# Regrouping the small matmuls of each expert in a mixture-of-experts block

## The chip, the cores and the metric

The kernel runs on one core of a Trainium2 chip. The time is device time in microseconds (us) of one execution, the median of three runs. The program is one launch.

## The reference, cut to what matters

The block is one layer of an encoder over 512 tokens of 1024 features in f32: pooling and differential attention, cross attention over 256 memory tokens, and then the part that the change touches, a mixture of 32 experts of which each token takes four:

```python
logits = (xt @ w_router + b_router)
top_val, top_idx = lax.top_k(logits, 4);  gates = softmax(top_val)
# for each expert e, on the tokens that chose it:
gu = xb @ w_gu[e] + b_gu[e]                      # (tokens, 2048)
gate, up = minimum(gu[:, :1024], 7), clip(gu[:, 1024:], -7, 7)
hb = (up + 1) * gate * sigmoid(1.702 * gate)     # (tokens, 1024)
yb = (hb @ w_down[e] + b_down[e]) * gate_of_token
y  = zeros.at[token].add(yb);   x = x + y;   out = rms_norm(x, g)
```

An expert has 64 tokens on average (512 x 4 / 32), and its weights are 12 MB, read once.

## The kernel before

The dense part fills the first 390 us or so; the change leaves it alone. The experts follow, in `experts` (L1173), one iteration per expert, and a last iteration (e = 32) for what is left.

An expert has up to 96 slots for its tokens: the first 64, and 32 more that run only if more than 64 tokens chose it. That choice is a branch at run time (`when`, L100, on a bit of a word that TensorE's sequencer has loaded; called `cond` in the loop). Experts with more than 96 tokens are finished by a loop at the end (`overflow`). An expert with over 64 tokens is called full in the prediction.

The products are in f32 with tokens as the columns of the weights' side: 64 slots take 64 columns of the array, and two such matmuls, for two halves of the output, stand beside each other in it; 32 slots take 32 columns, and four stand beside each other. `gate_up1` (L1086) is the product of one of eight pieces of the contraction in 64 columns, `gate_up2` (L1093) in 32. `down` (L1116) has `first(h)` in 64 columns for two halves h of the contraction, and `second(q, b)` in 32 columns for eight pieces.

Around these stand small jobs of TensorE, all with 128 columns:

- the slots (S): `dispatch` (L983) turns the places of the tokens into one-hots on VectorE and multiplies; out come the token numbers and gates of an expert's slots, which VectorE picks up in seven small instructions (`slots`, L966). The token rows are then gathered by an indirect DMA (`gather`, L989) into one buffer, and scaled on ScalarE (`normed`, L996);
- the transposes of the gathered tokens (T1): `to_features` (L1002), eight transposes into two banks, which VectorE writes to `xT` with the norm's gain in two halves; gate-up reads `xT`;
- the transposes of the activations (T2): `turn_act` (L1099), four and two, copied to `aT` by ScalarE; down reads them;
- the biases of gate-up (B): `biases` (L1068), four matmuls that start the sums;
- the pair's sums: `combine` (L1156). The outputs of down are split into two parts by `split` (L113), a ScalarE copy and then a VectorE subtraction for each piece, and kept for two experts (a pair). Then, for each of four blocks of 128 tokens, six matmuls with one-hots add the pair's outputs into two banks (`sum_up`), and VectorE adds these to x (`add_sums`, L1169).

The order on TensorE is the order of the program: `queued` (L88) hangs each matmul behind the one before it, branches included. On the other engines the framework's scheduler fixes an order ahead of time, from its own estimate of when each instruction is ready, the earlier one in the program first among the ready ones. Loads of weights are issued on the SP queue: `load_gate_up(e + 1)` and `load_down(e)` at the start of an iteration, each as soon as one of 17 buffers of 1 MB is free.

PSUM has eight banks: four single ones (`bank`, L137: slots, transposed activations, the 32-column part of gate-up, both parts of down), and two pairs (`pair`, L140: the 64-column part of gate-up, T1, and the sums).

Iteration e before the change, on TensorE: B; gate-up of 64 columns for pieces 0 to 7, with S (of expert e + 2) after piece 2, the first half of the 32-column part (if the expert is full) after piece 3, and T2 of expert e - 1 after piece 6. If e is odd and over 2, one of the four blocks of the sums of the last complete pair stands after each of the pieces 3 to 6. Then the second half of the 32-column part, T1 of expert e + 1, and down of expert e - 1: `first(0)`, the 32-column part, `first(1)`. In expert 1 the gate-weighted biases of down go into x in the places of the sums (`down_biases`, L944, then `combine`).

Of the kernel before, what the change touches and what calls it, by code (L numbers as in the profile page):

```python
# [15 lines left out]
OP = mybir.AluOpType  # L16
# [4 lines left out]
P = 128  # L21
D = 1024
S = 512
NT = S // P
KT = D // P
MEM = 256
NE = 32
# [33 lines left out]
class Block:  # L61
# [1054 lines left out]
    def down(self, aT, aT2, dn, gat, tok, cond, a, c, last=False):  # L1116


        (ya, oha), (yb, ohc) = a, c
        nc, mw = self.nc, self.mw  # L1120
        pd = [self.bank("down1") for _ in range(2)] if last else [self.bank("down1")] * 2
        pe = self.bank("down2", (P, 256))

        def first(h):
            for c in range(4):
                w = dn[2 * h + c // 2]
                for o in range(2):
                    k = D * (c % 2) + 512 * o
                    self.mm(pd[o][64 * o:64 * o + 64], aT[:, c, 64 * h:64 * h + 64], w[:, k:k + 512],
                            start=h == 0 and c == 0, stop=h == 1 and c == 3, skip_group_check=True)  # L1130

        def second(q, b):
            for o in range(4):
                k = D * b + 256 * o
                self.mm(pe[32 * o:32 * o + 32], aT2[:, b, 32 * q:32 * q + 32], dn[q][:, k:k + 256],
                        start=q + b == 0, stop=q == 3 and b == 1, skip_group_check=True)

        nc.vector.tensor_scalar(oha, self.iota_t, tok[:, 0:1], None, op0=OP.is_equal)
        nc.vector.tensor_scalar(ohc, self.iota_t[0:64], tok[0:64, 1:2], None, op0=OP.is_equal)
        if not last:  # L1140
            first(0)
        second(0, 0)
        with cond():
            for k in range(1, 8):
                second(k // 2, k % 2)
        for q in range(4):
            r, c = slice(32 * q, 32 * q + 32), slice(256 * (q % 2), 256 * (q % 2) + 256)
            self.split(yb[0:32, q // 2, c], yb[32:64, q // 2, c], pe[r], scale=gat[r, 1:2])
        if last:
            first(0)  # L1150
        first(1)
        for h in range(2):
            r = slice(64 * h, 64 * h + 64)
            self.split(ya[0:64, h], ya[64:P, h], pd[h][r], scale=gat[r, 0:1])

    def combine(self, i, parts):  # L1156

        nc = self.nc
        self.add_sums(i, self.sum_up(i, self.pair("comb"), parts, True, True))

    def sum_up(self, i, ps, parts, start, stop):
        t = slice(i * P, (i + 1) * P)
# [10 lines left out]
    def experts(self):  # L1173
        nc = self.nc
        disp, xTs, xgs = {}, {}, {}

        def gather(e):
            xgs[e] = self.gather(disp[e][0])

        def slots(e):  # L1180
            return [t[:, 0] for t in disp[e][1:]]

        xTs[0] = self.first_features()
        acts, parts = {}, {}
        pick = self.pick.rearrange("p v h q e -> p (v h q) e")
        for e in range(NE + 1):

            if e < NE:
                gu = self.gu.pop(e)
                cond = lambda e=e: self.when(self.flag(e))  # L1190
                if e == 0:
                    biases = self.load_down_biases()
                if e + 1 < NE:
                    self.load_gate_up(e + 1)
                    if e:
                        gather(e + 1)
                self.load_down(e)
                xT = xTs.pop(e)
                pa, pc = self.biases(pick[:, :, e:e + 1])
                for j in range(KT):  # L1200
                    self.gate_up1(pa, xT, gu[j], j)
                    if e == 0 and j == 0:
                        self.count()
                    if e == 0 and j == 1:
                        disp[1] = self.dispatch(1, 1)
                        gather(1)
                    if j == 3 or e == 0 and j in (1, 5):
                        with cond():
                            for k in range(j - 1 if e == 0 else 0, j + 1):
                                self.gate_up2(pc, xT, gu[k], k)  # L1210
                    if j in (3, 4, 5, 6) and e % 2 and e > 2:
                        self.combine(j - 3, parts[e // 2 - 1])
                    if j == 2 and e + 2 < NE:
                        disp[e + 2] = self.dispatch(e + 2, 1)
                    if j == 5 and e == 0:
                        disp[0] = self.dispatch(0, 1)
                        biases = self.round_down_biases(biases)
                    if e == 1 and j == 2:
                        biases = self.down_biases(biases)
                    if e == 1 and 2 < j < 7:  # L1220
                        self.combine(j - 3, [biases])
                    if j == 6 and e >= 1:
                        aT = [self.turn_act(t, n) for t, n in zip(acts.pop(e - 1), (4, 2))]
                    if j == 6 and e + 1 < NE:
                        xg = self.normed(xgs.pop(e + 1))
                if e:
                    act = self.swiglu(pa[:, 0], pa[:, 1], 512)
                with cond():
                    for k in range(4 if e else 6, KT):
                        self.gate_up2(pc, xT, gu[k], k)  # L1230
                if e == 0:
                    xTs[1] = self.to_features(xg)
                    act = self.swiglu(pa[:, 0], pa[:, 1], 512)
                acts[e] = act, self.swiglu(pc[:, 0], pc[:, 1], 256)
                if 0 < e < NE - 1:
                    xTs[e + 1] = self.to_features(xg)
            else:
                aT = [self.turn_act(t, n) for t, n in zip(acts.pop(e - 1), (4, 2))]

            if e:  # L1240
                f = e - 1
                r = slice(64 * (f % 2), 64 * (f % 2) + 64)
                if f % 2 == 0:
                    parts[f // 2] = self.sums()
                p = parts[f // 2]
                self.down(*aT, self.dnw.pop(f), *slots(f), lambda f=f: self.when(self.flag(f)),
                          p[2 * (f % 2)], [t[r] for t in p[1]], last=e == NE)
        self.finish(parts[NE // 2 - 1])
        self.overflow()
# [151 lines left out]
```

## Time and profile before

| what | us |
|---|---|
| median of 3 runs | 1530.26 (1529.31 to 1531.73) |
| the profiled execution | 1531.06 |
| its span, first to last instruction | 1529.3 |
| TensorE (PE) busy | 1482.5 (97% of the span) |
| weight loads (PEld) busy | 748.6 (49%) |
| VectorE (DVE) busy | 695.2 (45%) |
| ScalarE (ACT) busy | 385.1 (25%) |
| GpSimd (POOL) busy | 39.0 (3%) |

How to read it: the span is one execution; the time of an execution is a little longer. Busy time of an engine is the union of its instructions, and the matmuls' ends are modelled, so that a busy TensorE says that it has a matmul under way, not that it does as much as it could. A run of matmuls of one tile on the timeline is one row; an f32 matmul leaves two records in it. Idle time in brackets is that of the engine ahead of the row, with what ended it; PEq is TensorE's sequencer (here the branch).

### The profile page before, as it was taken

The page shows a single profiled execution, that of the slowest core. Times are in us where ns is not written, and L with a number is a line of the kernel's source. Part 1 is how long each engine was busy: PE and PEld are TensorE (multiplying, and loading weights), DVE is VectorE, ACT ScalarE, POOL GpSimd, SP SyncE. Part 2 cuts the span into 40 slices and gives each one's busy share as a digit, 9 for nine tenths or more (in the row PEclk, how much of TensorE's full clock was granted, in tenths as well). Part 3 has the DMA queues.
Part 4 walks back from the last instruction along what each step waited for, and adds up shares of the span by engine and source line. Part 5 has one row for each costly group of instructions (what it writes and reads, how often), then busy time and mean ns, then how long its engine had stood idle before and what let it go on. Part 6 is the DMA issues. An engine that isn't in the chain of part 4 may idle for free. (4 is left out here: it accounts for less than half of the span.)

```text
span 1529.3 us, 22025 instructions
## 1 busy us (share of the span) xinstructions
PE 1482.5 (97%) x8852; PEld 748.6 (49%) x8852; DVE 695.2 (45%) x1679; ACT 385.1 (25%) x691; POOL 39.0 (3%) x52
## 2 busy tenths in 40 slices
PE   8999999999999999999999999999999999999994
PEld 7878788888433333434333333333343433433332
DVE  6858865543353433335343334344343433444234
ACT  5346644441111111121211112121111112121113
POOL 0000000000000000000000000000000000000001
PEclk9999999999899999999999999999999999999997
DMA  6222225148778998989999998899989999999901
GB/s 221 90 86 88 106 63 175 80 196 318 273 304 341 387 398 318 369 356 373 396 405 408 407 381 344 343 400 367 395 342 386 387 393 370 364 396 387 416 25 57
DMA packets 84153, 455.38 MB, mean 298 GB/s; under 512 B 14169, under 2 KB 14690, under 8 KB 34882
## 3 DMA queue, kind: packets, MB, share of 16 engines
q1 hardware_dynamic: 79170, 438.90, 72.9%
q0 software_dynamic: 3472, 12.29, 2.5%
q10 hardware_dynamic: 1392, 2.51, 0.4%
q8 instruction: 87, 1.43, 0.4%
q14 instruction: 32, 0.26, 0.0%
HBM read 449.45 MB, written 4.21 MB: 297 GB/s over the span
## 5 line engine op out<-in xcount | busy, mean ns | idle before, releaser
L107 PE MATMUL gu<-gu,xT 128*64 128x512 f32 (+1 forms) x3200 | 602.7, 598 | 1.3 <-PEq L102 1.3
L107 PEld LDWEIGHTS gu<-gu,xT 128*64 128x64 f32 (+1 forms) x3200 | 167.7, 127 | 344.2 <-issue 337.3
L107 PE MATMUL down<-dnw,aT 128*32 128x256 f32 (+1 forms) x2288 | 305.3, 478 | 3.3 <-PEq L102 2.5
L107 PEld LDWEIGHTS down<-dnw,aT 128*32 128x32 f32 (+1 forms) x2288 | 109.1, 122 | 175.3 <-issue 149.6
L1105 ACT ACTIVATE aT<-actT 128x512 f32<-128x512 f32 x64 | 27.9, 487 | 542.2 <-PE actT L111 542.2
L1171 DVE TENSOR_TENSOR x<-comb,x 128x1024 f32<-128x1024 f32 x68 | 82.9, 1221 | 131.6 <-PE comb L107 131.6
L1059 DVE TENSOR_SCALAR g<-gu 128x256 f32<-128x256 f32 (+1 forms) x64 | 33.3, 554 | 229.1 <-PE gu L107 193.5
L121 DVE SCALAR_TENSOR_TENSOR yb<-down,gat,yb 32x256 fp32r<-32x256 f32 x128 | 61.6, 481 | 129.4 <-ACT yb L120 129.4
L120 ACT ACTIVATE yb<-down,gat 32x256 fp32r<-32x256 f32 x128 | 59.7, 466 | 224.3 <-PE down L107 118.2
L107 PE MATMUL comb<-ya,yb 128*128 128x512 f32 x256 | 97.0, 420 | 3.7 <-PEq L102 2.8
L107 PEld LDWEIGHTS comb<-ya,yb 128*128 128x128 f32 x256 | 47.9, 187 | 63.3 <-DVE x L1171 37.8
L118 DVE TENSOR_TENSOR w_lo<-w,w_hi 128x1024 fp32r<-128x1024 f32 x56 | 67.0, 1219 | 7.5 <-ACT w_hi L117 7.2
L121 DVE SCALAR_TENSOR_TENSOR ya<-down,gat,ya 64x512 fp32r<-64x512 f32 x64 | 48.0, 750 | 26.6 <-ACT ya L120 26.5
L970 DVE COPY slots<-slots 128x12 f32<-128x12 f32 x32 | 5.5, 171 | 118.3 <-PE slots L107 118.3
L117 ACT ACTIVATE w_hi<-w 128x1024 fp32r<-128x1024 f32 x56 | 56.6, 1052 | 5.6 <-DMA w<-in_w_ckv_dram 1.4
L1061 ACT ACTIVATE s<-g 128x256 f32<-128x256 f32 (+1 forms) x64 | 32.4, 521 | 87.6 <-DVE g L1059 85.8
L992 POOL DMA_INDIRECT xg<-x_rows,gi x31 | 28.6, 921 | 1004.2 <-DVE gu L1062 566.1
L120 ACT ACTIVATE ya<-down,gat 64x512 fp32r<-64x512 f32 x64 | 43.8, 685 | 32.6 <-DVE ya L121 23.9
L107 PE MATMUL comb<-yb,ohc 128*128 128x512 f32 x128 | 50.2, 393 | 0.0
L1065 DVE TENSOR_TENSOR g<-gu,s 128x512 f32<-128x512 f32 (+1 forms) x64 | 48.8, 842 | 0.0
L111 PEld LDWEIGHTS xgT<-ident,xg 96*128 96x128 f32 x248 | 29.9, 203 | 30.6 <-ACT xg L999 16.3
L999 ACT ACTIVATE xg<-xg 96x1024 f32<-96x1024 f32 x31 | 35.6, 1149 | 20.2 <-DMA xg<-x_rows,gi 19.5
(339 smaller groups left out, 1754.8 us busy)
## 6 DMA issues: line engine op xcount, KB each, us to landing
gu<-in_w_gu_dram SPq DMA_DIRECT2D x256, 1024.0 KB, 12.5
dnw<-in_w_down_dram SPq DMA_DIRECT2D x128, 1024.0 KB, 9.3
w<-in_w_ckv_dram SPq DMA_DIRECT2D x8, 1024.0 KB, 5.2
w<-in_w_in_dram SPq DMA_DIRECT2D x7, 1024.0 KB, 7.5
w<-in_w_out_dram SPq DMA_DIRECT2D x4, 1024.0 KB, 5.0
w<-in_w_cq_dram SPq DMA_DIRECT2D x4, 1024.0 KB, 7.8
w<-in_w_co_dram SPq DMA_DIRECT2D x4, 1024.0 KB, 5.1
x<-in_x_dram SPq DMA_DIRECT2D x8, 256.0 KB, 6.4
```

Source lines behind the costliest of these rows:

```text
L107: self.pin(self.nc.tensor.matmul(*a, **k))
L111: self.pin(self.nc.tensor.transpose(*a))
L117: self.pin(nc.scalar.activation(hi, src, AF.Copy))
L118: self.pin(nc.vector.tensor_tensor(lo, src, hi.bitcast(F32), op=OP.subtract))
L120: nc.scalar.activation(hi, src, AF.Copy, scale=scale)
L121: nc.vector.scalar_tensor_tensor(lo, src, scale, hi.bitcast(F32), op0=OP.mult, op1=OP.subtract)
L992: nc.gpsimd.indirect_dma_start(out=xg, out_offset=None, in_=self.rows, in_offset=bass.IndirectOffsetOnAxis(ap=gi, axis=0))
L999: self.nc.scalar.activation(xg[:, :D], xg[:, :D], AF.Copy, scale=xg[:, D:D + 1]))
L1059: nc.vector.tensor_scalar(g, gate, LIMIT, None, op0=OP.min)
L1061: nc.scalar.activation(s, g, AF.Sigmoid, scale=ALPHA)
L1065: nc.vector.tensor_tensor(g.rearrange("s (j b p) -> s j p b", p=P, b=2), r(up), r(s), op=OP.mult)
L1171: self.nc.vector.tensor_tensor(xi, ps, xi, op=OP.add)
```

## The change

Per iteration of expert e, the small jobs now come first and in one block: S of expert e + 2, T1 of expert e itself (and not of e + 1 at the end of the iteration), T2 of expert e - 1; then B and gate-up. The gate-up of 64 columns is interrupted only after piece 3, by all of a pair's sums (if e is odd and over 2) and by the first half of the 32-column part. The sums are made in halves of 512 features, eight for a pair, each with three matmuls in a single bank and an add of its own (`combine_half`), and not in pairs of banks. In down the 32-column part comes first and `first(0)`, `first(1)` follow each other, as the last expert had it before. Expert 1 adds the biases of down at the start of its iteration, ahead of S. In iteration 0 the slots of expert 2 are made after piece 2 as before, and T1 of expert 1 moves to iteration 1. The order of the loads' issue in the program is kept; the gather of expert e + 1 stands behind T1 of e.

```diff
@@ down
-        if not last:
-            first(0)
         second(0, 0)
         with cond():
...
             self.split(yb[0:32, q // 2, c], yb[32:64, q // 2, c], pe[r], scale=gat[r, 1:2])
-        if last:
-            first(0)
+        first(0)
         first(1)
@@ new
+    def combine_half(self, i, h, parts):
+        ps, n = self.bank("comb1"), len(parts)
+        for k, (y, oh) in enumerate(parts):
+            self.mm(ps, oh[:, i * P:(i + 1) * P], y[h] if isinstance(y, list) else y[:, h], start=k == 0,
+                    stop=k == n - 1, skip_group_check=True)
+        xi = self.x_sb[:, i, 512 * h:512 * h + 512]
+        self.nc.vector.tensor_tensor(xi, ps, xi, op=OP.add)
@@ experts, start of an iteration
+            if e == 0:
+                biases = self.load_down_biases()
+            if e == 1:
+                biases = self.down_biases(biases)
+                for i in range(NT):
+                    self.combine(i, [biases])
+            if 0 < e < NE - 2:
+                disp[e + 2] = self.dispatch(e + 2, 1)
+            if 0 < e < NE:
+                xTs[e] = self.to_features(xg)
+            if e:
+                aT = [self.turn_act(t, n) for t, n in zip(acts.pop(e - 1), (4, 2))]
@@ experts, amid gate-up
+                    if j == 3 and e % 2 and e > 2:
+                        for i in range(NT):
+                            for h in range(2):
+                                self.combine_half(i, h, parts[e // 2 - 1])
                     if j == 3 or e == 0 and j in (1, 5):
                         with cond():
...
-                    if j in (3, 4, 5, 6) and e % 2 and e > 2:
-                        self.combine(j - 3, parts[e // 2 - 1])
-                    if j == 2 and e + 2 < NE:
-                        disp[e + 2] = self.dispatch(e + 2, 1)
+                    if e == 0 and j == 2:
+                        disp[2] = self.dispatch(2, 1)
...
-                    if e == 1 and j == 2:
-                        biases = self.down_biases(biases)
-                    if e == 1 and 2 < j < 7:
-                        self.combine(j - 3, [biases])
-                    if j == 6 and e >= 1:
-                        aT = [self.turn_act(t, n) for t, n in zip(acts.pop(e - 1), (4, 2))]
@@ experts, end of gate-up
-                if e:
-                    act = self.swiglu(pa[:, 0], pa[:, 1], 512)
+                act = self.swiglu(pa[:, 0], pa[:, 1], 512)
...
-                if e == 0:
-                    xTs[1] = self.to_features(xg)
-                    act = self.swiglu(pa[:, 0], pa[:, 1], 512)
                 acts[e] = act, self.swiglu(pc[:, 0], pc[:, 1], 256)
-                if 0 < e < NE - 1:
-                    xTs[e + 1] = self.to_features(xg)
-            else:
-                aT = [self.turn_act(t, n) for t, n in zip(acts.pop(e - 1), (4, 2))]
```

## Rows read from the trace of the kernel before

**Rows 1.** Table of stretches: us, busy time of each engine, granted clock, DMA share, GB/s

```profile
600.00:1480.00 880.00, 870.29 (x5224) 337.16 (x5222) 347.11 (x793) 158.58 (x279) 21.96 (x24) 1.00 0.93 370
760.00:860.00 100.00, 98.41 (x555) 38.79 (x554) 43.90 (x99) 17.71 (x32) 2.75 (x3) 1.00 1.01 404
```

**Rows 2.** Timeline of TensorE, expert 28: start, us, what, [idle before, releaser]

```profile
1349.21 5.37 PE L107 MATMUL gu<-gu,xT 128*64 128x512 f32 x24
1354.52 0.35 PE L107 MATMUL slots<-tv,oh 128*128 128x6 bf16 x8
1354.80 1.94 PE L107 MATMUL gu<-gu,xT 128*64 128x512 f32 x8
1357.05 5.37 PE L107 MATMUL gu<-gu,xT 128*64 128x512 f32 x24 [0.31 <-PEq L102]
1362.35 0.87 PE L111 MATMUL actT<-ident,g 128*128 128x128 f32 x6
1363.15 1.94 PE L107 MATMUL gu<-gu,xT 128*64 128x512 f32 x8
1365.40 1.10 PE L111 MATMUL xgT<-ident,xg 96*128 96x96 f32 x8 [0.31 <-PEq L102]
1366.43 4.22 PE L107 MATMUL down<-dnw,aT 128*64 128x512 f32 x24
```

**Rows 3.** Timeline of TensorE, expert 27: visits of a pair's sums

```profile
1324.88 0.50 PE L107 MATMUL comb<-ya,yb 128*128 128x512 f32 x1
1325.22 0.40 PE L107 MATMUL comb<-yb,ohc 128*128 128x512 f32 x1
1325.45 0.63 PE L107 MATMUL comb<-ya,yb 128*128 128x512 f32 x2
...
1326.48 1.94 PE L107 MATMUL gu<-gu,xT 128*64 128x512 f32 x8
...
1331.81 0.50 PE L107 MATMUL comb<-ya,yb 128*128 128x512 f32 x1
...
1333.30 0.82 PE L111 MATMUL actT<-ident,g 128*128 128x128 f32 x6
```

**Rows 4.** Timeline of the weight loads (PEld): down of expert 26, biases of 28

```profile
1340.90 3.18 PEld L107 LDWEIGHTS down<-dnw,aT 128*32 128x32 f32 x64 [0.81 <-issue]
1344.50 0.20 PEld L107 LDWEIGHTS down<-dnw,aT 128*64 128x64 f32 x4 [0.41 <-issue]
...
1348.08 0.77 PEld L107 LDWEIGHTS gu<-bias,lh 128*128 128x128 f32 x4 [0.81 <-issue]
```

**Rows 5.** Page, costliest groups: down; count | busy, mean ns | idle before

```profile
L107 PE MATMUL down<-dnw,aT 128*32 128x256 f32 (+1 forms) x2288 | 305.3, 478 | 3.3 <-PEq L102 2.5
```

**Rows 6.** Groups by line and form, VectorE: an add of 512 elements

```profile
L484 DVE TENSOR_TENSOR x<-ops,x 128x512 f32<-128x512 f32 x8 | 5.5, 686 | 8.1 <-PE ops L107 8.0
```

**Rows 7.** Timeline of ScalarE and VectorE around the end of a down

```profile
1348.26 0.69 ACT L120 ACTIVATE ya<-down,gat 64x512 fp32r<-64x512 f32 x1
1348.98 0.74 DVE L121 SCALAR_TENSOR_TENSOR ya<-down,gat,ya 64x512 fp32r<-64x512 f32 x1 [0.26 <-ACT ya L120]
...
1349.75 0.36 DVE L1074 CAST lh<-pick 128x384 fp32r<-128x384 f32 x1
...
1350.47 0.76 DVE L121 SCALAR_TENSOR_TENSOR ya<-down,gat,ya 64x512 fp32r<-64x512 f32 x1 [0.36 <-ACT ya L120]
...
1369.38 1.01 DVE L1010 TENSOR_TENSOR xT<-xgT,g_ffn 128x384 f32<-128x384 f32 x2
```

**Rows 8.** Timeline of VectorE, expert 28: first and last of 11 for the slots

```profile
1354.91 0.17 DVE L970 COPY slots<-slots 128x12 f32<-128x12 f32 x1 [3.68 <-PE slots L107]
...
1356.20 0.28 DVE L961 TENSOR_SCALAR oh<-iota,slot_no 128x256 bf16<-128x256 bf16 x1
```

**Rows 9.** Timeline, expert 1: transposes of the gates, last write of gT

```profile
424.24 0.60 PE L111 MATMUL gT<-ident,gate 128*32 128x128 f32 x4
...
425.94 0.68 DVE L953 TENSOR_TENSOR gT<-gT 32x512 fp32r<-32x512 f32 x1
```

More of the change, by code (lines that the diff above doesn't have):

```diff
@@ L1183, in experts @@
         xTs[0] = self.first_features()
-        acts, parts = {}, {}
+        acts, parts, xg = {}, {}, None
         pick = self.pick.rearrange("p v h q e -> p (v h q) e")
         for e in range(NE + 1):
+            if e == 0:
[10 more added lines that the diff above has]
+                aT = [self.turn_act(t, n) for t, n in zip(acts.pop(e - 1), (4, 2))]
             if e < NE:
@@ L1190, in experts @@
                 cond = lambda e=e: self.when(self.flag(e))
-                if e == 0:
-                    biases = self.load_down_biases()
                 if e + 1 < NE:
@@ L1230, in experts @@
                         self.gate_up2(pc, xT, gu[k], k)
-                if e == 0:
-                    xTs[1] = self.to_features(xg)
-                    act = self.swiglu(pa[:, 0], pa[:, 1], 512)
                 acts[e] = act, self.swiglu(pc[:, 0], pc[:, 1], 256)
-                if 0 < e < NE - 1:
-                    xTs[e + 1] = self.to_features(xg)
-            else:
-                aT = [self.turn_act(t, n) for t, n in zip(acts.pop(e - 1), (4, 2))]
             if e:
```

## The prediction

> **What bounds the kernel now.** I read the table of stretches first: from 600 to 1480 us, where 26 of the 32 experts run, TensorE is busy 98.9% of the time at a granted clock of 1.00 (2.4 GHz), VectorE 39% and ScalarE 18% [rows 1]. So the end is set by TensorE's list, which is issued in written order, and an edit is worth what it takes out of that list or makes it wait. The second row is the densest stretch for the DMA: 404 GB/s against 370 on average [rows 1]. A list 3% shorter asks for some 383 on average, below 404, and I charge the weights nothing.
>
> Then the timeline of TensorE alone, where each row is one run of like matmuls. An f32 matmul leaves two records. Expert 28 has few tokens. Its gate-up in 64 columns runs 24 records in 5.37 us and 8 in 1.94, so one more record is (5.37 - 1.94) / 16 = 0.214 us. From the start of the 24 to the start of what follows are 5.31 us (1349.21 to 1354.52), 24 x 0.214 are 5.15, and **the rest, 0.15 us, is what each interruption of a column run costs**, whatever comes in between [rows 2]. The guests themselves take, from start to start: slots (S) 0.28, act transposes (T2) 0.80, token transposes (T1) 1.03 [rows 2], biases (B) 1.13 (1348.08 to 1349.21) [rows 2, 4]. Where a branch is taken TensorE is empty for 0.31 us ahead of the next run [rows 2].
>
> In expert 27 the pair's sums come in four visits of six matmuls. A visit takes 1.60 us (1324.88 to 1326.48); inside it the beat is 0.23 (1325.22 to 1325.45), six beats are 1.39, so entry and exit cost 0.21. The last visit, followed by T2 and not by a column run, takes 1.49 (1331.81 to 1333.30): **two guests side by side are 0.11 cheaper than apart** [rows 3].
>
> In the down product the weight loads show the forms: the 32-column part begins at 1340.90, the second 64-column part at 1344.50, the biases at 1348.08. The last 16 records take 3.58; at 0.214 they are 3.43, so 0.15 is again the break [rows 4].
>
> 2288 records of down in all are 32 x 40 plus 18 x 56: 18 experts have over 64 tokens and run all of the 32-column work [rows 5].
>
> **The change part by part.** Expert 1 apart, 30 experts (2 to 31) gain, half of them with a pair's sums.
>
> Gate-up of an even expert is now interrupted by S and T2; both go: 2 x 0.15 = 0.31. In an odd one S and four visits interrupt it (T2 rides on the last); one visit stays: 4 x 0.15 = 0.61. The branch around the 32-column part stays in either.
>
> Sums: 24 matmuls in one visit, so three entries and exits go, 3 x 0.21 = 0.63, and the join with T2, 0.11, goes with them: 0.52. This needs VectorE to keep up: a half's add of 128x512 takes 0.69 [rows 6], TensorE needs 3 x 0.23 = 0.69 for a half, and three of the four single banks are free then (one holds the gate-up of 32 columns). Two halves of slack hide small waits; I charge nothing, at most 8 x 0.1 us in 15 experts, 12 us. Better than nothing it can't be.
>
> Down in two runs and not three: one break, 0.15. In the full experts, 18 at most, the 32-column gate-up now runs straight into the 32-column down. No row shows such a meeting: between nothing and a break of 0.15; I take 0.07, the middle, since it is the same form but another bank, 1.3 us in all.
>
> S, T1, T2 and B stand side by side: three joins. The nearest row is the 0.11 above; ends are 0 and a full break, 0.15. 3 x 0.11 = 0.33.
>
> Sum: even 0.31 + 0.15 + 0.33 = 0.79, odd 0.61 + 0.52 + 0.15 + 0.33 = 1.61; 15 x 0.79 + 15 x 1.61 + 1.3 = **37 us gained** (with the ends of joins and meeting: 26 to 42).
>
> The Trainium skill, TensorEngine Tiling (Array Packing), Key Properties, says that a change of tiling mode, and not a change of tile alone, drains the array. The breaks of 0.15 agree with it. By that rule the meeting of equal forms is free, and the gain is 1.4 us larger; no run here shows it yet.
>
> *What it costs.* First, **T1 loses its cover.** T1 was followed by two or three runs of down, 7.2 to 10.8 us at 3.6 each [rows 4], under which VectorE brought the features (xT) to SBUF. Now only T2 and B lie between T1 and the gate-up that reads xT. From the end of down (T0) TensorE needs 0.28 + 1.03 + 0.80 + 1.13 less three joins = 2.9 us, and the first half of xT must be there. That write is 0.54 us, as two take 1.01 with their overlap [rows 7]. What else is queued at VectorE: two evictions of down, each behind its ScalarE copy. Set against T0 = 1348.08: ScalarE copies from 0.18 to 0.87, VectorE evicts from 0.90 to 1.64, waits for ScalarE's second copy and evicts from 2.39 to 3.15 [rows 7]. S moves there too, and its eleven small instructions (seven for the slots, four one-hots for the next) take 1.57 (1354.91 to 1356.48) [rows 8]. VectorE is free before 0.90 and from 1.64 to 2.39. The first gap takes about half of S's, the second the rest of the seven (0.5), then xT at 2.15 to 2.7: just in time. If it comes behind all of this without a pause it ends at 0.39 + 1.57 + 1.50 + 0.54 = 4.0, with 0.1 for the signal 1.2 late; if at once, not late. So 0 to 1.2 per expert; I take 0.15, for the gap of 0.75 is wide enough for 0.5 and a start of xT: 30 x 0.15 = 4.5 us (0 to 36). The gather of the next tokens waits for T1 on its one buffer, and T1 now stands behind the down that it stood ahead of; the gather is issued about 1.3 us after T0, a whole gate-up and down ahead of its own T1, and costs nothing.
>
> Second, **expert 1.** The biases of down (gate transposes, then four sums) stood amid its gate-up; now they stand ahead of it with nothing behind them. From the transposes to the last write of gT are 2.38 us (424.24 to 426.62), of which TensorE works some 0.5 [rows 9]. Then four sums in two pairs of banks, each held by an add of 1024 elements, at most 2 x 0.69 [rows 6]: 5.5 us, under which TensorE has some 4 us of its own (sums, S, T1, T2). 1.85 + 1.5 = 3.3 lost, 1.6 gained as in other odd experts: net about 1.5, ends 0 and 4 (if the activation of expert 0 is ahead on VectorE).
>
> Third, two branches now stand close: gate-up, branch, 8 records in 32 columns, branch, 64 columns. The second wait was hidden in part by what ran before; 0 to 0.13 in 14 experts, I take 1 us.
>
> Everything that issues DMAs stays in its order on the SP queue. The first two tiles of down come free after 7.2 of 10.8 us before, and after 3.6 + 3.4 = 7.0 now; gate-up's first four come some 4 us later in odd experts, which the average rate can bear.
>
> Together: 1531.06 (the profiled execution; the span is 1529.3) - 37.3 + 4.5 + 1.5 + 1 = 1500.8. The median of the runs is 0.8 lower, so **1500 us**.
>
> **Rivals.**
> - *xT behind both evictions.* VectorE works in the order of its list, fixed ahead of time; if xT is listed after the second eviction it starts at 3.15, ends at 3.7, and gate-up is 0.9 late: 27 in place of 4.5 us, **1522**. For it: xT stands later in the program than the evictions. Against: between the two evictions VectorE's list already holds work from further on in the program, the cast of the next expert's lh at 1349.75 [rows 7]. 0.22.
> - *The other side: xT behind the evictions and all of S's instructions.* 3.15 + 1.57 + 0.54 + 0.1 = 5.4, 2.45 late, 30 x 2.45 = 73 us: **1569**. It decides from 1.2 us per expert on. For it: S now precedes T1 in the program. Against: the small instructions have two gaps to go to. 0.06.
> - *Joins and meeting are worth nothing*: 10 + 1.3 us less, **1511**. Against it the visit of 1.49. 0.07.
> - *The clock falls.* The stretch of S, T1, T2 and B has no column run in 2.9 us. If TensorE were granted 1.2 GHz in it, it would take twice as long: 30 x 2.9 = 87, **1587**. Against: T1 and T2 already stand in every expert of a stretch granted 1.00 throughout [rows 1]. 0.03. The Trainium skill, TensorE: Matmul & The Clock Gate, Part 4, says that transposes don't count as busy for the clock as matmuls do; the trace shows no fall by them so far.
>
> **How the numbers follow.** The forecast has 0.62. Its own range, with joins and the charge for xT between 0 and 0.4, is 1491 to 1513. The range of 8 in 10 goes up to the first rival, 1491 to 1523; outside stay the two slow rivals (0.09), half of the first's spread above (0.06) and less than 0.05 below. A measurement of this kernel can tell 0.2%, 3 us, from nothing. Faster: the forecast, the joins' rival and nearly all of the first, 0.88; within 0.2%, a charge for xT near 1.2: 0.05; slower 0.07.
>
> **What would show it.** In the profile after, TensorE's timeline should have S, T1, T2, B in one piece of about 2.9 us from the end of down to gate-up, a visit of 24 sums of 5.7, gate-up runs of 32 records, and down in two runs. A wait ahead of gate-up released by VectorE's xT shows the first rival; its length times 30 is the loss. Waits inside the 24 sums on VectorE's add would show the single banks too few. If the cycle of an even expert falls by much less than 0.8 us without such waits, the 0.15 is not what an interruption costs, and the forecast is wrong at its root.

## The result, and the profile after

The changed kernel takes 1502.42 us (median of 4 runs, 1501.17 to 1503.90) against 1530.99 for the kernel before, timed beside it (1529.31 to 1532.32): a ratio of 0.9816 (0.9803 to 0.9828), 28.6 us faster. Its profiled execution took 1501.75 us, with a span of 1500.0. The forecast was 1500.

First the table of stretches of the changed kernel: us, busy time and instructions of PE, PEld, DVE, ACT and POOL, granted clock, DMA share, GB/s. The first row answers to [rows 1], the others are the start of expert 1.

```profile
600.00:1450.00 850.00, 840.23 (x5238) 355.90 (x5238) 356.01 (x830) 159.72 (x275) 21.89 (x24) 1.00 0.96 385
...
413.80:419.60 5.80, 0.59 (x8) 0.28 (x5) 5.47 (x10) 1.52 (x3) 0.00 (x0) 0.86 0.97 388
419.60:426.00 6.40, 4.39 (x8) 2.16 (x8) 4.96 (x6) 0.00 (x0) 0.00 (x0) 0.50 0.02 6
426.00:431.20 5.20, 5.17 (x28) 4.08 (x28) 3.39 (x17) 0.87 (x2) 0.91 (x1) 0.50 0.11 17
```

In the long stretch TensorE is as full as before (98.9%) at the same clock, and the DMA moves 385 GB/s in place of 370, close to the 383 that a shorter list asked for. So the gain there is a shorter list, as forecast. In expert 1 the table shows something new: the granted clock is 0.50 (1.2 of 2.4 GHz) from 419.6 to 431.2.

TensorE's timeline of the changed kernel, experts 27 and 28 (start, us, what; the sums of expert 27 are among the lines left out):

```profile
1281.60 7.09 PE L107 MATMUL down<-dnw,aT 128*64 128x512 f32 x32 [0.18 <-PEq L102]
1288.62 0.35 PE L107 MATMUL slots<-tv,oh 128*128 128x6 bf16 x8
1288.83 1.11 PE L111 MATMUL xgT<-ident,xg 96*128 96x96 f32 x8
1289.78 0.82 PE L111 MATMUL actT<-ident,g 128*128 128x128 f32 x6
1290.36 1.17 PE L107 MATMUL gu<-bias,lh 128*128 128x512 f32 x4
1291.67 7.09 PE L107 MATMUL gu<-gu,xT 128*64 128x512 f32 x32
...
1324.44 1.18 PE L107 MATMUL gu<-bias,lh 128*128 128x512 f32 x4
1325.63 7.09 PE L107 MATMUL gu<-gu,xT 128*64 128x512 f32 x32
```

The block is there in one piece: S 0.21, T1 0.95, T2 0.58, B, and gate-up in runs of 32 records without a guest. From gate-up to gate-up, expert 27 takes 33.96 us (1291.67 to 1325.63). Before it took 35.59: its gate-up began at 1313.62, that of expert 28 at 1349.21 [rows 2]:

```profile
1313.62 5.37 PE L107 MATMUL gu<-gu,xT 128*64 128x512 f32 x24
```

Read in the same way from all starts of gate-up in the two traces, the cycle of an even expert (2 to 30) falls by 0.64 to 1.12 us, median 0.82, and that of an odd one (3 to 29) by 1.63 to 1.95, median 1.65. The prediction had 0.79 and 1.61 before its charge for xT, and an even cycle that falls by much less than 0.8 was its sign of being wrong at the root: that sign did not come.

VectorE, ScalarE and the weight loads around one such block of the changed kernel, ahead of expert 25:

```profile
1224.01 0.74 DVE L121 SCALAR_TENSOR_TENSOR ya<-down,gat,ya 64x512 fp32r<-64x512 f32 x1
...
1225.19 0.56 DVE L1010 TENSOR_TENSOR xT<-xgT,g_ffn 128x384 f32<-128x384 f32 x1
...
1225.80 0.20 PEld L107 LDWEIGHTS gu<-gu,xT 128*64 128x64 f32 x4 [0.57 <-DVE xT L1010]
...
1226.31 0.76 DVE L121 SCALAR_TENSOR_TENSOR ya<-down,gat,ya 64x512 fp32r<-64x512 f32 x1
```

xT comes ahead of the second eviction (1225.19 against 1226.31), so the first rival's order is not the one that was drawn. But the weight load of gate-up does wait for xT. The view of waits shows nothing of it, since the matmuls' modelled ends cover the gap. It is read from the starts: from B to gate-up are 1.31 us here (1224.49 to 1225.80) and in 1290.36 to 1291.67, 1.19 in 1324.44 to 1325.63; where nothing is late (experts 30 and 31) they are 1.11. So the wait is 0.20 after an even expert and 0.08 after an odd one; it stands in 26 of the 30 blocks, and 2, 29, 30 and 31 have none.

The start of expert 1 in the changed kernel, TensorE first, then VectorE:

```profile
413.78 0.61 PE L111 MATMUL gT<-ident,gate 128*32 128x128 f32 x4
419.63 2.04 PE L107 MATMUL comb<-b_down,gT 96*128 96x512 f32 x4 [5.24 <-DVE gT L953]
422.14 2.35 PE L107 MATMUL comb<-b_down,gT 96*128 96x512 f32 x4 [0.47 <-DVE x L1177]
426.00 0.88 PE L107 MATMUL slots<-tv,oh 128*128 128x6 bf16 x8 [1.52 <-DVE oh L961]
...
429.20 2.05 PE L107 MATMUL gu<-bias,lh 128*128 128x512 f32 x4
431.19 5.14 PE L107 MATMUL gu<-gu,xT 128*64 128x512 f32 x22
```

```profile
413.91 1.02 DVE L1059 TENSOR_SCALAR g<-gu 128x256 f32<-128x256 f32 x2 [3.18 <-PE gu L107]
...
418.35 0.42 DVE L952 CAST gT<-gT 32x512 fp32r<-32x512 f32 x1
418.80 0.68 DVE L953 TENSOR_TENSOR gT<-gT 32x512 fp32r<-32x512 f32 x1
420.86 2.35 DVE L1177 TENSOR_TENSOR x<-comb,x 128x1024 f32<-128x1024 f32 x2 [1.38 <-PE comb L107]
```

VectorE does all of expert 0's activation (413.91 to 418.35) ahead of gT, and TensorE, with gT's sums next in its list, stands for 5.24 us. Then it waits 0.47 amid the sums and 1.52 for the one-hots of S: 7.2 us idle in all. The gate-up of expert 1 begins at 431.19 in place of 418.72, 12.5 us later. The same place in the kernel before:

```profile
417.63 1.16 PE L107 MATMUL gu<-bias,lh 128*128 128x512 f32 x4 [1.21 <-DVE xT L1010]
418.72 5.37 PE L107 MATMUL gu<-gu,xT 128*64 128x512 f32 x24
```

So the two spans differ by 29.3 us in three pieces, all from the starts of gate-up. Up to expert 0's gate-up the profiled execution after is 1.5 us early, a piece that the change does not touch and that falls anywhere from 1.7 early to 1.8 late in the profiled executions of the experiments. Expert 1's gate-up comes 13.99 later against expert 0's, and expert 2's gets 3.90 back: **+10.1 us, where the forecast had +1.5**. From there to the end **37.9 us are gained, where the forecast had 37.3 - 4.5 - 1 = 31.8**. Some 0.8 us of both pieces is no loss and no gain: S and T2 of expert 2's block (0.21 + 0.58) now stand ahead of its gate-up, and so ahead of the border between the pieces, where before they stood behind it.

### The profile page after: what moved, and what is told of

The parts are those of the page before. It is cut to its first block, busy times and chain, and to the rows that moved or that the text cites. A ratio compares the mean times of both kernels' runs of the same rounds, so it can differ in the third digit from the quotient of the medians.

```text
span 1500.0 us, 22053 instructions
## 1 busy us (share of the span) xinstructions
PE 1446.5 (96%) x8852; PEld 771.7 (51%) x8852; DVE 709.3 (47%) x1739; ACT 388.6 (26%) x691; POOL 38.9 (3%) x52
## 5 line engine op out<-in xcount | busy, mean ns | idle before, releaser
L107 PE MATMUL gu<-gu,xT 128*64 128x512 f32 (+1 forms) x3200 | 582.6, 595 | 4.8 <-PEq L102 1.5
L107 PEld LDWEIGHTS gu<-gu,xT 128*64 128x64 f32 (+1 forms) x3200 | 180.8, 127 | 381.4 <-issue 360.3
L1059 DVE TENSOR_SCALAR g<-gu 128x256 f32<-128x256 f32 x64 | 32.7, 552 | 396.9 <-PE gu L107 287.1
L107 PEld LDWEIGHTS down<-dnw,aT 128*32 128x32 f32 (+1 forms) x2288 | 120.6, 122 | 183.5 <-issue 148.4
L1061 ACT ACTIVATE s<-g 128x256 f32<-128x256 f32 x64 | 33.5, 523 | 395.4 <-DVE g L1059 394.9
L1165 DVE TENSOR_TENSOR x<-comb,x 128x512 f32<-128x512 f32 x120 | 82.7, 689 | 91.6 <-PE comb L107 91.0
L107 PE MATMUL comb<-ya,yb 128*128 128x512 f32 x256 | 85.5, 404 | 0.9 <-DVE x L1177 0.9
L1065 DVE TENSOR_TENSOR g<-gu,s 128x256 f32<-128x256 f32 x64 | 49.2, 843 | 3.0 <-ACT s L1061 3.0
L1105 ACT ACTIVATE aT<-actT 128x512 f32<-128x512 f32 x64 | 31.2, 490 | 43.6 <-PE actT L111 42.9
L107 PE MATMUL gu<-bias,lh 128*128 128x512 f32 x128 | 39.4, 431 | 0.0
L111 PE MATMUL xgT<-ident,xg 96*128 96x96 f32 x248 | 34.8, 284 | 0.0
```

Of the source, the lines that this page charges most:

```text
L107: self.pin(self.nc.tensor.matmul(*a, **k))
L111: self.pin(self.nc.tensor.transpose(*a))
L1059: nc.vector.tensor_scalar(g, gate, LIMIT, None, op0=OP.min)
L1061: nc.scalar.activation(s, g, AF.Sigmoid, scale=ALPHA)
L1065: nc.vector.tensor_tensor(g.rearrange("s (j b p) -> s j p b", p=P, b=2), r(up), r(s), op=OP.mult)
L1105: nc.scalar.activation(aT, pt[:, :n], AF.Copy)
```

## The experiments

The theory after the result was: the list is shorter by the steps of the prediction; expert 1 loses 10 us because its biases of down stand at its start. The rivals: another part carries the gain, the xT wait is worth removing, or expert 1's loss comes from the block itself. Ratios are to the kernel before on the same chip.

### a_bias_back: the biases of down amid expert 1's gate-up again

```diff
-            if e == 1:
-                biases = self.down_biases(biases)
-                for i in range(NT):
-                    self.combine(i, [biases])
...
+                    if e == 1 and j == 2:
+                        biases = self.down_biases(biases)
+                    if e == 1 and 2 < j < 7:
+                        self.combine(j - 3, [biases])
```

> The changed kernel, but in expert 1 the biases of down go back amid the gate-up, as before the change. Theory (expert 1 lost some 10 us because its biases stood at the head with nothing behind them: a wait of 5.2 us for gT, 1.5 us for the one-hots that share gT's buffer, adds one after another, and a slower TensorE after these waits): about 9.8 us less than the 1502.4 of the changed kernel, 1493. Rival (the 14 us that expert 1's cycle grew by are mostly work moved from the next cycle, which fell by 3.9, and slots and transposes that must run anyway): 1500 or more.

Measured: 1497.15 us, 0.9776 (0.9762 to 0.9789), 5 us better than the change and not 10. Part of expert 1's loss stays. TensorE there:

```profile
420.35 1.51 PE L111 MATMUL actT<-ident,g 128*128 128x128 f32 x6 [3.23 <-DVE slots L970]
```

T2 needs a bank that S holds until VectorE copies the slots, and that copy stands behind the same activation. And the granted clock is 0.50 here too (stretches, columns as above):

```profile
419.80:423.20 3.40, 2.85 (x10) 2.33 (x10) 1.89 (x10) 0.39 (x1) 0.00 (x0) 0.50 0.88 324
```

### b_gates_early: the gates' transposes already in expert 0

```diff
             if e == 1:
-                biases = self.down_biases(biases)
                 for i in range(NT):
                     self.combine(i, [biases])
...
+                    if e == 0 and j == 6:
+                        biases = self.down_biases(biases)
```

> The changed kernel, but the gates' transposes and the writes of gT stand in expert 0 after piece 6 of its gate-up; the sums of the biases stay at the head of expert 1. It tells the wait for gT from the adds. Theory (the wait for gT is half of the loss in expert 1): 5.2 us less, less 0.7 for the interruption in expert 0, and little or no slow stretch after it: 1502.4 - 6 = 1496.5. Rival (the adds behind the activation on VectorE set the end anyway): 1501 to 1502.

Measured: 1501.35 us, 0.9808 (0.9793 to 0.9823), the rival's number. gT is early now, and the sums of the first block run at once. The next sums wait until the activation's last operation (L1065) has let go of a pair of banks, and the adds on VectorE stand behind the activation too:

```profile
414.42 0.74 PE L107 MATMUL comb<-b_down,gT 96*128 96x512 f32 x2
418.98 2.18 PE L107 MATMUL comb<-b_down,gT 96*128 96x512 f32 x4 [3.82 <-DVE g L1065]
...
424.22 0.88 PE L107 MATMUL slots<-tv,oh 128*128 128x6 bf16 x8 [1.51 <-DVE oh L961]
```

In the change, in a and in b, whatever of TensorE's list first asks VectorE for something meets expert 0's activation.

### j_expert1_old: a, and expert 1's S and T2 back in their old places

```diff
-            if 0 < e < NE - 2:
+            if 1 < e < NE - 2:
                 disp[e + 2] = self.dispatch(e + 2, 1)
...
-            if e:
+            if e > 1:
                 aT = [self.turn_act(t, n) for t, n in zip(acts.pop(e - 1), (4, 2))]
...
-                    if e == 0 and j == 2:
-                        disp[2] = self.dispatch(2, 1)
+                    if e < 2 and j == 2:
+                        disp[e + 2] = self.dispatch(e + 2, 1)
...
+                    if j == 6 and e == 1:
+                        aT = [self.turn_act(t, n) for t, n in zip(acts.pop(e - 1), (4, 2))]
```

> As a_bias_back, and in expert 1 the slots and the act transposes too go back amid the gate-up, as before the change. Theory (in expert 1 the block has no down ahead of it: its T2 waited 3.2 us for a bank that the slots' copy behind the activation of expert 0 held, and TensorE was slower after it): the way from T1 to gate-up shrinks from 7.6 to the 3.4 of before, less 1.4 for the two interruptions: 2.8 us less than 1497, 1494. Rival (T1 and B wait for the activation all the same): 1497.

Measured: 1497.61 us, 0.9782 (0.9769 to 0.9795), not to be told from a. The wait moved once more, to B, which begins at 421.68 after 3.43 us for the activation's last operation. In the kernel before TensorE waited 1.21 us at this place, for xT, which stood second in VectorE's list, after the activation's first operation. The change moved T1 behind expert 0's activation (the diff's "end of gate-up"), and a, b, j, k and l all keep that. Putting the activation back behind T1 was not run, so that this order is the rest of expert 1's loss is argued from the waits and not shown.

### l_warm_wait: 80 matmuls of no use in the wait for gT

```diff
                 biases = self.down_biases(biases)
+                self.warm(80)
                 for i in range(NT):
```

> The changed kernel with 80 more small matmuls (bf16, 128 columns, their result unused) in expert 1 between the gates' transposes and the sums, where TensorE was idle for 5.24 us. Theory (that idle time made the granted clock fall to 1.2 GHz, and the slow slots, T1, T2, biases and first gate-up of expert 1 are its price): these run at their usual times, some 3 us less, 1499.4, if the other waits there don't make it fall. Rival (the slow instructions wait for VectorE and banks, not for the clock): 1502.4, and granted clock or not they take as long.

Measured: 1502.47 us, 0.9815 (0.9800 to 0.9830): no gain. Its stretches (columns as above):

```profile
414.00:420.80 6.80, 6.03 (x96) 4.97 (x89) 5.50 (x10) 1.52 (x3) 0.00 (x0) 1.00 0.99 404
420.80:426.40 5.60, 2.65 (x8) 1.26 (x8) 4.83 (x6) 0.00 (x0) 0.00 (x0) 0.93 0.03 9
426.40:431.60 5.20, 5.14 (x26) 4.06 (x26) 3.41 (x17) 0.87 (x2) 0.91 (x1) 0.50 0.10 16
```

With the wait filled, the clock stays at 1.00 up to 420.8. Then TensorE is busy for 2.65 of 5.6 us, with waits of 0.85, 0.39 and 1.72 us, and the block again runs at 0.50, with T1 taking 1.32 us from start to start and B 1.98. The 0.50 goes with these durations, but its price alone wasn't separated: no run with the new block kept it away from expert 1.

### c_down_only: the kernel before, with the new order in down

```diff
-        if not last:
-            first(0)
         second(0, 0)
...
-        if last:
-            first(0)
+        first(0)
         first(1)
```

> The kernel before, with the 32-column part of down ahead of the two 64-column runs and nothing else. Theory (each interruption of a column run costs 0.15 us): 31 x 0.15 = 4.7 us less than 1531, 1526.3. Rival (the break is free, the later first run gives it back): 1531.

Measured: 1525.60 us, 0.9971 (0.9960 to 0.9983). In the trace the cycle of an expert is shorter by 0.15 us, the price of one break, in nearly all of them.

### d_sums_only: the kernel before, with one visit in halves

```diff
+                    if j == 3 and e % 2 and e > 2:
+                        for i in range(NT):
+                            for h in range(2):
+                                self.combine_half(i, h, parts[e // 2 - 1])
...
-                    if j in (3, 4, 5, 6) and e % 2 and e > 2:
-                        self.combine(j - 3, parts[e // 2 - 1])
```

> The kernel before, with the pair's sums in one visit after piece 3, in halves in single banks, and nothing else. T2 then interrupts gate-up alone. Theory: per odd expert two interruptions less (0.31) and three entries and exits less (0.63), one meeting with T2 lost (0.11 to 0.14): 15 x 0.82 = 12.3 us less, 1518.5. Rival (VectorE's adds of 0.69 us for each 0.69 of TensorE don't keep up): a wait of some 0.1 us per half, 15 x 8 x 0.1 = 12 us given back, 1531.

Measured: 1519.12 us, 0.9921 (0.9905 to 0.9938). Odd experts lose 0.73 or 0.86 us each. T2 now interrupts gate-up by itself: at 1256.22 it stands between runs of 24 and 8 records.

### e_block_only: the kernel before, with the block alone

It is a without the new order of down and with the sums in four visits of pairs:

```diff
+        if not last:
+            first(0)
         second(0, 0)
...
-        first(0)
+        if last:
+            first(0)
         first(1)
...
-                    if j == 3 and e % 2 and e > 2:
-                        for i in range(NT):
-                            for h in range(2):
-                                self.combine_half(i, h, parts[e // 2 - 1])
+                    if j in (3, 4, 5, 6) and e % 2 and e > 2:
+                        self.combine(j - 3, parts[e // 2 - 1])
```

> The kernel before, with S, T1 and T2 in one block with the biases, and nothing else (down in three runs, sums in four visits in pairs of banks, the biases of down in visits). Theory: even experts lose two interruptions (0.31) and three joins (0.39) and wait 0.05 for xT, 0.65; odd ones lose one interruption (0.15) and three joins, give up the join of T2 with the sums (0.14) and wait 0.13, 0.27; 15 x 0.92 = 14 us less, 1517. Rival (T1 without the cover of down costs what the block gains): 1531.

Measured: 1524.94 us, 0.9963 (0.9951 to 0.9975): 8 us above what was expected. The view of TensorE's waits from 600 to 1480 us in it (us in total, times, longest), and from its timeline the gate-up of one expert:

```profile
PE gu L107 <- DVE xT L1010: 6.0, 20, 0.5
```

```profile
1241.00 2.37 PE L107 MATMUL gu<-gu,xT 128*64 128x512 f32 x10 [0.22 <-DVE xT L1010]
```

From expert 6 to 28, B to gate-up takes 1.40 to 1.66 us here, where the full change has 1.31 and 1.19. Over experts 2 to 31 that is 5.0 us more. In the block shown, the last eviction of down's 32-column part ends 0.42 us behind the start of S, where the change has 0.32, and xT starts 0.08 later. That the old order of down is the reason in the others too is argued from this and not shown.

The three parts give 5 + 11 + 6 = 22 us, and together (a) 34. Each leaves something that only the others take away. With d alone T2 keeps an interruption, and with e alone the fourth visit does: 15 x 0.15 = 2.3. T2's meeting with the sums is lost in d and again in e, and only once with both: 15 x 0.11 = 1.7. The 32-column runs meet only with c and e together: 18 x 0.11 = 2.0. And e alone has 5.0 more of xT's wait. That is 11.0 of the 12, worked out from rows and not by a run of their own.

### f_pairs_one_visit and g_halves_four_visits: the two halves of the new sums

f keeps one visit and goes back to pairs of banks, g keeps the halves and goes back to four visits; both stand on a.

```diff
 # f
-                            for h in range(2):
-                                self.combine_half(i, h, parts[e // 2 - 1])
+                            self.combine(i, parts[e // 2 - 1])
 # g
-                    if j == 3 and e % 2 and e > 2:
-                        for i in range(NT):
-                            for h in range(2):
-                                self.combine_half(i, h, parts[e // 2 - 1])
+                    if j in (3, 4, 5, 6) and e % 2 and e > 2:
+                        for h in range(2):
+                            self.combine_half(j - 3, h, parts[e // 2 - 1])
```

> As a_bias_back, with the pair's sums in one visit, but in pairs of banks as before (an add of 1024 elements), of which gate-up holds one, so that a single pair is free. Theory (the halves in single banks are what lets the sums stand side by side): each of the last three blocks waits for the add of the one before it, 1.22 + 0.1 us, 15 x 3 x 1.33 = 60 us more than 1497, 1557. Rival (one visit is all that counts): 1497.

> The changed kernel with expert 1's biases back amid the gate-up, and the pair's sums in halves in single banks, but in four visits after pieces 3 to 6 and not in one. Theory (grouping is what gains): per odd expert three interruptions (0.46) and three entries and exits (0.63) more, 15 x 1.09 = 16 us more than 1493, 1509. Rival (single banks and halves are what gains): 1493.

Measured: f 1567.94 us, 1.0240 (1.0224 to 1.0255), slower than the kernel before; g 1513.18 us, 0.9886 (0.9870 to 0.9901). The waits of f from 600 to 1480 us:

```profile
PE comb L107 <- DVE x L1177: 47.4, 36, 1.3
```

Each pair after the first waits 1.32 us for an add of 1024 elements, three times in a visit. From one pair's start to the next's, in f's timeline:

```profile
1279.82 0.50 PE L107 MATMUL comb<-ya,yb 128*128 128x512 f32 x1
...
1282.80 0.50 PE L107 MATMUL comb<-ya,yb 128*128 128x512 f32 x1 [1.32 <-DVE x L1177]
```

These are 2.98 us, where six beats are 1.39 [rows 3]. So a wait costs nearly 1.6 and not the 1.33 of the expectation: the modelled ends hide the rest. 15 x 3 x 1.59 = 72, and f is 71 us above a, 11 more than expected. So one visit pays only with halves in single banks. The other way round, g is 16 us above a, which is 15 times three entries and exits and three breaks (0.63 + 0.46). Whether halves in four visits gain anything on pairs in four visits was not run.

### h_t1_first and i_t1_last: T1 ahead of S, and T1 behind the biases

Both stand on a. In i the gather goes with T1.

```diff
 # h
-            if 0 < e < NE - 2:
-                disp[e + 2] = self.dispatch(e + 2, 1)
             if 0 < e < NE:
                 xTs[e] = self.to_features(xg)
+            if 0 < e < NE - 2:
+                disp[e + 2] = self.dispatch(e + 2, 1)
 # i
-            if 0 < e < NE:
-                xTs[e] = self.to_features(xg)
...
+                pa, pc = self.biases(pick[:, :, e:e + 1])
+                if e:
+                    xTs[e] = self.to_features(xg)
+                    if e + 1 < NE:
+                        gather(e + 1)
                 xT = xTs.pop(e)
-                pa, pc = self.biases(pick[:, :, e:e + 1])
```

> As a_bias_back, and T1 ahead of S in the block, so that xT has the time of S more. Theory (the biases' 1.31 us in odd and 1.19 in even experts, against 1.11 where gate-up does not wait, are the wait for xT): 15 x 0.20 + 15 x 0.08 = 4 us less than a_bias_back, 1489, and TensorE's biases take 1.11 everywhere. Rival (VectorE's list is drawn up anew and puts xT behind the second eviction of down): 0.8 x 30 = 24 us more, 1517.

> As a_bias_back, but T1 stands last in the block, behind the biases, so that nothing covers the write of xT. Theory (T2 and B are the cover of xT, 1.7 us of it): gate-up waits at least 0.26 us (half of T1 0.5, then 0.1 + 0.55 of VectorE against T1's 0.94), and up to 1.0 where the second eviction of down is ahead: 1493 + 30 x 0.26 to 1.0, 1501 to 1523, I take 1508. Rival (xT needs no cover): 1493, as a_bias_back.

Measured: h 1504.35 us, 0.9822 (0.9809 to 0.9836), 7 us slower than a; i 1563.76 us, 1.0209 (1.0193 to 1.0224). h was expected 4 us faster than a, and i at 1508. In h xT is early and yet gate-up starts late:

```profile
1224.34 1.02 DVE L1010 TENSOR_TENSOR xT<-xgT,g_ffn 128x384 f32<-128x384 f32 x2
...
1225.28 0.16 DVE L970 COPY slots<-slots 128x12 f32<-128x12 f32 x1
1225.29 0.30 PEld L107 LDWEIGHTS gu<-bias,lh 128*128 128x128 f32 x2 [0.50 <-ACT aT L1105]
...
1225.96 0.20 PEld L107 LDWEIGHTS gu<-gu,xT 128*64 128x64 f32 x4 [0.37 <-issue]
```

The slots' copy stands behind xT in VectorE's list now, so the bank of S is still full when the second half of B asks for one of the four single banks. It gets one that T2 holds, and waits 0.50 us for the ScalarE copy that empties it (aT, 0.60 us from 1224.64). In a the same place has no wait. From B to gate-up are 1.44 and 1.38 us here, and 1.31 and 1.19 in a: the wait for xT has become a wait for a bank, and is longer. In i the wait is the one of the prediction's other side:

```profile
1212.02 0.76 DVE L121 SCALAR_TENSOR_TENSOR ya<-down,gat,ya 64x512 fp32r<-64x512 f32 x1
...
1212.81 1.02 DVE L1010 TENSOR_TENSOR xT<-xgT,g_ffn 128x384 f32<-128x384 f32 x2
...
1213.42 1.94 PE L107 MATMUL gu<-gu,xT 128*64 128x512 f32 x8 [1.83 <-DVE xT L1010]
...
1249.00 13.36 PE L107 MATMUL gu<-gu,xT 128*64 128x512 f32 x68 [1.70 <-DVE xT L1010]
```

xT is behind all of S's instructions, the cast of lh and both evictions. The view of waits has 42.9 us in 25 such waits from 600 to 1480, 1.7 each, which is 51 us in 30 experts; from S to gate-up a block is some 1.65 longer than in a, 49 in 30. i is 67 us above a. Much of the rest is the clock. A stretch of i, right behind the wait that ends at 1249.00:

```profile
1249.00:1253.00 4.00, 4.00 (x12) 1.29 (x14) 0.41 (x1) 0.00 (x0) 0.00 (x0) 0.57 1.03 409
```

The clock did not fall behind every such wait. In the 4 us behind it, the granted clock is 0.57 to 0.64 in 12 of the 30 experts and 1.00 in the other 18. At 1213.42 above, after 1.83 us, 8 records take 1.94 us, as at full clock [rows 2]. A cycle with the fall is 1.4 to 1.7 us longer than its like without, some 20 us in all. What decides between the 12 and the 18 no run here shows.

### k_slots_last: j, and S behind the biases

```diff
-            if 1 < e < NE - 2:
-                disp[e + 2] = self.dispatch(e + 2, 1)
...
                 pa, pc = self.biases(pick[:, :, e:e + 1])
+                if 1 < e < NE - 2:
+                    disp[e + 2] = self.dispatch(e + 2, 1)
```

> As j_expert1_old, with the slots last in the block, behind the biases, in place of first. In h_t1_first the biases waited for a bank that the slots' copy, listed behind xT on VectorE, still held; here the slots ask for a bank last, and cover xT like the others. Theory (xT's and the bank's waits are both gone): the biases take 1.1 us everywhere, 15 x 0.20 + 15 x 0.08 = 4 us less than j_expert1_old, 1490. Rival (four single banks: the slots themselves wait for one): as much as j_expert1_old or more, 1494 to 1500.

Measured: **1494.23 us**, 0.9764 (0.9750 to 0.9778), the best kernel of this study; its interval lies below that of the change. The block of expert 25 in it, TensorE:

```profile
1213.65 1.13 PE L111 MATMUL xgT<-ident,xg 96*128 96x96 f32 x8
1214.62 0.82 PE L111 MATMUL actT<-ident,g 128*128 128x128 f32 x6
1215.20 1.18 PE L107 MATMUL gu<-bias,lh 128*128 128x512 f32 x4
1216.22 0.35 PE L107 MATMUL slots<-tv,oh 128*128 128x6 bf16 x8
1216.50 1.94 PE L107 MATMUL gu<-gu,xT 128*64 128x512 f32 x8
```

2.85 us from T1 to gate-up, the sum of the four without any wait: xT no longer stands behind S's small instructions, and B waits for no bank. Against j the cycles are 0.20 and 0.08 shorter, the two waits for xT read above. So those waits cost the change 13 x 0.28 = 3.6 us, and they were there to be had: the medians of j and k lie 3.4 apart.

## Why the prediction was right, and where it was not

**The bound and the sum.** TensorE's list did set the end, and shortening it by interruptions shortened the time. The two errors, 8.6 us too little for expert 1 and 6.1 too little gained elsewhere, nearly cancel: that the forecast came within 2.4 us of the median with two terms off is luck. Without the 0.8 that crossed the border the errors are some 7.8 and 5.3; of the 5.3, the joins are 1.8, the two branches 1.0, xT 0.9 and the meeting 0.7, and the rest is not told apart. The upper end of the forecast's own range, 1513, does not follow from its terms: joins at nothing and 0.4 us for xT add 10 and 7.5 to 1500, which is 1517.

**Break of 0.15.** Shown: c takes away one per expert, and nearly every cycle is 0.15 shorter.

**Sums in one visit.** The visit of 24 takes 5.79 us for 5.7 in the full experts (6.0 in the others, with a branch behind it), with no wait on the single banks. d and g show that the number of visits counts as the prediction put it, and f that the single banks are needed.

**Joins.** The block takes 0.22 + 0.94 + 0.58 + 1.11 = 2.85 us without a wait, against 3.24 apart [rows 2, 4]: 0.39 for 0.33.

**Meeting of 32-column runs.** Forecast at 0.07 gained, of 0.15. Both 32-column runs of gate-up in expert 30 and the start of down behind them (weight loads and matmuls in one timeline of the changed kernel):

```profile
1395.40 0.16 PEld L107 LDWEIGHTS gu<-gu,xT 128*32 128x32 f32 x8 [0.81 <-issue]
...
1398.97 0.20 PEld L107 LDWEIGHTS gu<-gu,xT 128*64 128x64 f32 x4 [0.84 <-issue]
...
1405.99 0.16 PEld L107 LDWEIGHTS gu<-gu,xT 128*32 128x32 f32 x8 [0.81 <-issue]
...
1409.45 5.08 PE L107 MATMUL down<-dnw,aT 128*32 128x256 f32 x70
```

The run that 64 columns follow takes 3.57 us (1395.40 to 1398.97), the one that meets down 3.46 (1405.99 to 1409.45). The last of these is the start of the matmul; its weight loads begin at 1409.02, ahead of it. So the meeting saves 0.11 of the break's 0.15, and costs some 0.04. The rule of the Trainium skill, TensorEngine Tiling (Array Packing), Key Properties, that a change of mode and not of tile drains the array, agrees with this trace but for the 0.04: equal form and another bank cost 0.04, another form 0.15.

**Two close branches.** Charged at 1 us. The 8 records of 32 columns take 0.79 to 0.81 and the next branch 0.18 (1281.60), as before: nothing to charge.

**xT.** Charged at 0.15 per expert between 0 and 1.2, for a start between the two evictions. That place is the one drawn, and the waits are 0.08 and 0.20. Rival one's order did not come. i shows the order of the other side's rival in a kernel a step away from the change, at 1.7 to 1.8 us each, where the prediction had 2.45. That i took 1563.76 in all, near the prediction's 1569, is chance: some 20 us of it is the clock, which that rival did not have.

**Expert 1: the step that was mis-sized.** The prediction had 1.5 us (0 to 4; its terms as written, 1.85 + 1.5 - 1.6, give 1.75): "5.5 us, under which TensorE has some 4 us of its own (sums, S, T1, T2)". But these four stand behind gT's wait in TensorE's own list, so they cover nothing of it; they run after it. The measured account is 7.2 us idle (5.24 + 0.47 + 1.52), 2.3 us more for the block at the granted clock of 0.50 (5.19 from S to gate-up in place of 2.85), some 1.8 more for the sums themselves (4.4 busy in place of 4 x 0.64), less the 1.6 gained: 9.7 of the 10.1. Two terms that this leaves out nearly cancel: the 1.21 us that the kernel before waited for xT here are gone, and 0.8 crossed the border, which makes 9.3. Two things were missed. The activation of expert 0 was named as an end of the range and was in fact ahead on VectorE for 4.4 us. And the waits went with a lower clock, which the prediction had not counted here; l did not separate its price.

**The clock.** The rival of a fall in every block did not come: with S, T1, T2 and B in one piece the clock is 1.00 from 600 to 1450. In the experts it fell only where waits stood, in expert 1 and in i, and not behind all of them. The Trainium skill, TensorE: Matmul & The Clock Gate, Part 4, has it that transposes don't count as busy for the clock in the same way as matmuls; with T1 and T2 side by side for 1.5 us in each block this trace shows no fall by them.

## What to carry to other kernels

On an engine with a full, ordered list, count its interruptions: a price per interruption read from one timeline (0.15 us) gave the gain of the down order and of the sums, each done alone, to within 1 us, and parts that share an interruption are worth more together than apart. Work hides a wait only if it stands ahead of the waiting instruction in that engine's list; what stands behind it is delayed, however much of it there is. When a producer moves close to its consumer, look at the list of the engine between them, and move what is small and not urgent (S here) behind the consumer's other needs.

## What the runs showed of the hardware that was not expected

The granted clock fell to 0.50 with short waits, but not with each: with 3.23 us in a, and in i with 1.70 us ahead of gate-up, where the next 4 us ran at 0.57 on average. In i that happened behind 12 of 30 waits of the same length. In f, 36 waits of 1.32 us left the clock at 1.00 from 600 to 1480, and so did the blocks of the change without such a wait from 600 to 1450: each took 2.66 to 3.05 us.

Making one operand early can bring out a wait for a PSUM bank: in h, with xT 0.85 us earlier than in the change (1224.34 against 1225.19; both blocks begin at 1222.74 or 1222.75), gate-up began later, at 1225.96 against 1225.80.

The weights begin to show: k has five waits of TensorE for the DMA from 600 to 1480 us, 1.6 us together, where the changed kernel has one of 0.3. Whether a list much shorter still would wait for them more was not run.
